# A hybrid decoder step on one core: token tiles normed in pairs, half of w_out split ahead into DRAM, output tiles beside attention's end

## The chip, the core and the metric

The kernel runs on one core of one Trainium2 chip. The metric is the device time of one execution in microseconds (us); lower is better. The engines are TensorE (PE, matmuls and transposes), VectorE (DVE), ScalarE (ACT), GpSimd (POOL) and SyncE (SP, which here only issues DMA transfers). Each engine works through its own instructions in order and waits on semaphores for the others.

## What is computed

One step of a decoder layer for a new sequence of 1024 tokens (d_model 1024) and for 8 sample tokens with a past of 2048, all in float32. In short:

```python
h = rms_norm(x, norm_g)
b_gate, c_gate, conv_in, z_conv, q, kv, gate_logits, z_attn = split(h @ w_in)
q = rope(rms_norm(q, q_gain)) / 8            # 8 heads of 64
k = rope(rms_norm(kv[..., 0, :, :], k_gain)) # 3 branches, 2 kv heads
o = g0 * attn(q, compress_blocks(kv_cmp)) + g1 * attn(q, top 16 blocks of kv_slc) \
    + g2 * attn(q, last 512 of kv_win)
y = x + concat(b_gate * short_conv(c_gate * conv_in) * silu(z_conv), o * silu(z_attn)) @ w_out
```

For the samples the compressed and selected branches read a paged cache through `page_table`. The key and value rows of the new tokens, the window state and the conv state are outputs too.

## The kernel before

**Matmuls.** A float32 operand is split into a high and a low part of type fp32r (`copy` on ACT makes the high part, `sub`, L78, on DVE or POOL the low part), and a product is three matmuls: high by high, high by low, low by high. `tok_mm` (L201) makes a tile of 128 tokens by 256 columns with 8 × 3 matmuls (L208 to L210), `chan_mm` (L216) a block of 128 channels by 384 tokens (L223 to L225). There are nine token tiles; the ninth holds the 8 samples.

**First stage.** `phase0` (L530) makes, in this order: the normed and transposed input `hH`, `hL` (`x_load`, `x_norm`, `turn_x`), the key and value rows of the compressed branch (weights `c0`), of the selected branch (`c1`), the compressed blocks of the new sequence (L599, from `XH`, `XL`), the rows of the window branch (`c2`), and the queries in two halves of 256 columns (`which`). `norm_rope` (L253) norms a tile's heads and turns them: squares on ACT (one instruction per head with accumulation for keys, one for a query tile, then a DVE reduction L259), the root in `rsqrt` (L189: one ACT and four small DVE steps, L194 to L197), and the products on DVE (L267, L270, L273, L275). `twice` (L277) doubles the keys into `kd`, and transposes put them into `K` (`k_finish`, L483) or, for the compressed branch, into `XH`, `XL` (`cmp_transposes`, L403). `posted` runs such work a set number of tiles later. Weights of the next pass are loaded on SP (`wraw`, L169) and split (`wh` on ACT, `wl` on POOL) while a pass runs. `x_load` has three buffers, so SP waits until a tile has been normed and transposed before it can load the fourth.

**Order of work.** `merge` (L30) interleaves two generators by the costs that they yield: `phase0` with weight 150 and `z_part`, blocks of the gate channels (`chan_stream`, L315), with weight `ZW` = 43. After that `first` (attention, then the output tiles) is merged with `second` (the other channel blocks and the convolution, `prefetch`, the sample's compressed cache, the sample's attention). A scheduler of the framework then places the instructions on the engines, which can move them past one another where data allows.

**Attention** (`attn_stream`, L754) has 32 units: 8 query tiles, 2 kv heads, 2 pairs of query heads. A unit makes scores on PE (L796), a masked softmax on DVE and ACT (L784, L786), scales the probabilities by a statistic and the gate on POOL (`scale`, L841 and L845), transposes them (L870), splits them into `ph`, `pl`, and multiplies by the values (L880). `finish` adds the result into `mixA`. The last units have the longest rows.

**Output.** `prefetch` (L1340) loads the eight pieces of the first half of `w_out` (`w_piece`, L1326, tile `wor`) and the compression weights `cwr`, and splits them on ACT and DVE, beside attention's last units. `out_stream` (L1360) makes 16 output tiles of 128 tokens by 512 columns, 24 matmuls each (L1405 to L1407), once attention is over; `cmp_stream` (L972) then gathers the sample's cache (L981, 16 indirect gathers of 1 MB through POOL's queue, two buffers), regroups it (`reg`), transposes (L999) and compresses it (L1023).

Of the kernel before, what the change touches and what calls it, by code (L numbers as in the profile page):

```python
# [1 line left out]

# [58 lines left out]
def hymba_step_kernel(ctx, tc, io):  # L61
    nc = tc.nc
    WARM = 24
# [55 lines left out]
    mixA = mixp.tile([128, 4, NTOK], F32, name="mixA")  # L119
    mCf = mixC.rearrange("p a c -> p (a c)")  # L120
# [3 lines left out]
    kv1p = left.enter_context(pool("kv1"))  # L124
    K, V = {}, {}

    K[1] = kv1p.tile([128, 2, 32 + SEQ], F32R, name="k1")
    kpc = K[1][:, :, 0:32]
    KOFF = {1: 32, 2: 0}
    V[1] = kv1p.tile([128, 8, 2, 128], F32R, name="v1")  # L130
# [16 lines left out]
    warm = ps.tile([128, 512], F32, name="cc", tag="cc", bufs=2)  # L147
    for _ in range(WARM):
        PE.matmul(warm[:, :256], vpc[:, 0], vpc.rearrange("p g c -> p (g c)"), start=True, stop=True)

    banks = {"mm": [(ps, "mm", 3)], "tp": [(ps, "tp", 3)], "cc": [(ps, "cc", 2)]}
# [9 lines left out]
    def w_loader(wp, n, kp, raw_bufs, hk, hl_bufs, lo_eng=POOL):  # L161


        def load(col, width):
            hs, ls, raws = [], [], []

            def fetch(i, home=wp):
                r = home.tile([128, kp, n], F32, name="wraw", bufs=raw_bufs)
                SP.dma_start(r[:, :, :width], w_in[:, i * kp:(i + 1) * kp, col:col + width])  # L169
                raws.append(r)  # L170

            def split(i, eh=ACT, el=lo_eng):
                for j in range(0, kp, hk):
# [4 lines left out]
                    sub(el, l[:, :, :width], r, f(h[:, :, :width]))  # L178
# [22 lines left out]
    def tok_mm(t, w, n):  # L201

        o = bank("mm")
# [47 lines left out]
    E2 = [(DVE, DVE), (DVE, DVE), (DVE, DVE), (DVE, DVE)]  # L251

    def norm_rope(wk, src, n, t, nh, ct, sn, ea=DVE, eb=DVE):  # L253
        w = nh * 64
        sq = wk.tile([128, 256], F32, name="sq")
        ss = wk.tile([128, 8], F32, name="ss", bufs=4)
        if nh == 4:
            ACT.activation(sq[:n, :w], src, AF.Square, scale=0.125)
            DVE.tensor_reduce(ss[:n, :nh], sq[:n, :w].rearrange("p (h d) -> p h d", h=nh), axis=AX, op=OP.add)  # L259
        else:  # L260
            for h in range(nh):
                c = slice(h * 64, h * 64 + 64)
                ACT.activation(sq[:n, c], src[:, c], AF.Square, scale=0.125, accum_out=ss[:n, h:h + 1])
        r = rsqrt(wk, ss[:n, :nh], n, nh)
        qn = wk.tile([128, 4, 64], F32, name="qn")
        q = qn[:n, :nh]
        DVE.tensor_tensor(q, src.rearrange("p (h d) -> p h d", h=nh), r[:, :, None].to_broadcast([n, nh, 64]), OP.mult)  # L267
        a = wk.tile([128, 4, 64], F32, name="ra")
        b = wk.tile([128, 4, 64], F32, name="rb")
        ea.tensor_tensor(a[:n, :nh], q, ct[:n, t][:, None, :].to_broadcast([n, nh, 64]), OP.mult)  # L270
        for i in range(2):
            o, s = slice(32 * i, 32 * i + 32), slice(32 - 32 * i, 64 - 32 * i)
            eb.tensor_tensor(b[:n, :nh, o], q[:, :, s],  # L273
                               sn[:n, t, o][:, None, :].to_broadcast([n, nh, 32]), OP.mult)
        DVE.tensor_tensor(src.rearrange("p (h d) -> p h d", h=nh), a[:n, :nh], b[:n, :nh], OP.add)  # L275

    def twice(wk, rows, n):  # L277

        kd = wk.tile([128, n, 2, 64], F32, name=f"kd{n}", tag="cwr" if n == 4 else "kd2", bufs=CWR if n == 4 else 3)
        v = rows[:, :n * 64].rearrange("p (a d) -> p a d", a=n)  # L280
        copy(DVE, kd, v[:, :, None, :].to_broadcast([128, n, 2, 64]))
        return kd

    def kv_rows(wk, o, t, br, ct, sn):

        if t < 8:
            n, src = 128, o
# [5 lines left out]
        if br == 2:  # L293
            copy(ACT, gates[:n, t, :], src[:n, 256:280])
# [1230 lines left out]
```

## Time and profile before

| | us |
|---|---|
| Median of 3 runs | 936.41 (935.55 to 942.97) |
| The profiled execution | 939.33 |
| Span of its profile, first to last instruction | 937.6 |
| Mean granted clock of TensorE in it | 0.976 of full speed |

Shares of busy time, stretches, waits and chains below are of the profiled execution, on the scale of its span, from 0 to 937.6 us. A busy PE is not PE at its peak, since matmuls overlap and their ends are modelled. In this execution the first key tile begins some 10 us in, the queries are made from about 170 to 236 us, attention runs to about 674 us, and the sample's stages with the output tiles follow.

### The profile page before, as it was taken

Reading aid. Unit: us, or ns where it says so; the run is one execution under the profiler, and the core shown is the slowest. Engines: PE = TensorE matmul, PEld = TensorE weight load, DVE = VectorE, ACT = ScalarE, POOL = GpSimd, SP = SyncE. Lnnn points to the kernel's source line nnn. Section 1 sums busy time; section 2 is a strip of 40 time slices with the busy share of each in tenths; the row PEclk is TensorE's granted clock in tenths of the full one; section 3 lists DMA queues with packets and bytes.
Section 4 is the critical chain, followed back from the end, with each engine's and each line's share of the span. In section 5 each row is a group of like instructions: output and inputs, shape, how many; then the busy total and the mean of one; then the engine's idle time right before and its main releaser. Section 6 shows DMA issues by size and latency. Waiting matters only on the chain.

```text
span 937.6 us, 16976 instructions
## 1 busy us (share of the span) xinstructions
PE 873.8 (93%) x5789; PEld 783.2 (84%) x5789; DVE 619.4 (66%) x1714; ACT 556.0 (59%) x1495; POOL 404.3 (43%) x550
## 2 busy tenths in 40 slices
PE   7988999999899999999989999999679999798998
PEld 6888999999689889898979899998568888576765
DVE  5896734788655555856775686577745555877883
ACT  5764543733665655656556666576757666675761
POOL 4132340311454444444434444343455543477761
PEclk8999989999999999999999999999989999899999
DMA  7513331211011000000000100001495661857631
GB/s 246 154 57 95 95 114 35 80 57 31 6 30 34 24 23 24 23 24 23 13 12 23 24 23 1 23 2 44 127 302 182 214 214 47 314 179 226 214 102 47
DMA packets 57955, 82.24 MB, mean 88 GB/s; under 512 B 14470, under 2 KB 43086, under 8 KB 55692
## 3 DMA queue, kind: packets, MB, share of 16 engines
q1 hardware_dynamic: 50956, 47.60, 16.9%
q0 software_dynamic: 6912, 33.56, 10.6%
q8 instruction: 46, 0.75, 0.3%
q14 instruction: 41, 0.34, 0.1%
HBM read 74.24 MB, written 11.10 MB: 91 GB/s over the span
## 4 chain that ended last, share of the span: by engine, by line
PE 49%; ACT 7%; DVE 7%; POOL 3%; issue 3%; DMA 1%; ACTq 0%; DVEq 0%; POOLq 0%
PE o L880 7%; PE pt L870 5%; PE s L796 5%; PE mm L225 5%; PE mm L224 5%; PE mm L223 5%; POOL P L845 2%; ACT P L786 2%; PE mm L1407 1%; PE pt L999 1%; PE mm L1405 1%; PE mm L1406 1%; PE mm L1023 1%; ACT ph L75 1%; PE o L1278 1%
## 5 line engine op out<-in xcount | busy, mean ns | idle before, releaser
L223 PE MATMUL mm<-hH,wh 128*128 128x384 f32 (+1 forms) x480 | 157.9, 329 | 0.0
L225 PE MATMUL mm<-hH,wl 128*128 128x384 f32 (+1 forms) x480 | 155.7, 324 | 0.0
L224 PE MATMUL mm<-hL,wh 128*128 128x384 f32 (+1 forms) x480 | 155.1, 323 | 0.0
L786 ACT ACTIVATE P<-P,stat 128x640 f32<-128x640 f32 (+7 forms) x192 | 112.9, 590 | 37.4 <-DVE stat L784 36.8
L79 POOL TENSOR_TENSOR wl<-wraw,wh 128x256 fp32r<-128x256 f32 (+1 forms) x120 | 87.7, 749 | 106.2 <-ACT wh L75 96.8
L79 DVE TENSOR_TENSOR pl<-pt,ph 128x512 fp32r<-128x512 f32 (+1 forms) x164 | 102.4, 636 | 45.3 <-ACT ph L75 43.9
L75 ACT ACTIVATE ph<-pt 128x512 fp32r<-128x512 f32 (+1 forms) x164 | 88.3, 549 | 66.1 <-PE pt L870 65.5
L845 POOL TENSOR_SCALAR P<-P,stat,gates 128x640 f32<-128x640 f32 (+7 forms) x128 | 101.1, 800 | 55.8 <-DVE stat L836 52.7
L870 PE MATMUL pt<-ident,P 128*128 128x128 f32 x592 | 95.5, 278 | 6.4 <-POOL P L845 3.5
L796 PE MATMUL s<-k,q 128*128 128x320 f32 (+8 forms) x416 | 95.8, 334 | 3.7 <-DVE q L79 1.5
L208 PE MATMUL mm<-wh,hH 128*128 128x256 f32 (+1 forms) x320 | 93.5, 292 | 0.4 <-ACT hH L75 0.4
L209 PE MATMUL mm<-wl,hH 128*128 128x256 f32 (+1 forms) x320 | 93.2, 292 | 0.2
L210 PE MATMUL mm<-wh,hL 128*128 128x256 f32 (+1 forms) x320 | 93.0, 291 | 0.0
L223 PEld LDWEIGHTS mm<-hH,wh 128*128 128x128 f32 x480 | 91.9, 191 | 0.8 <-DVE mixC L693 0.6
L224 PEld LDWEIGHTS mm<-hL,wh 128*128 128x128 f32 x480 | 91.9, 191 | 0.1
L225 PEld LDWEIGHTS mm<-hH,wl 128*128 128x128 f32 x480 | 91.9, 192 | 0.1
L784 DVE CUSTOM_DVE_ANT_0 P<-s,mask 128x32 f32<-128x32 f32 (+8 forms) x160 | 70.9, 473 | 27.0 <-PE s L796 22.4
L870 PEld LDWEIGHTS pt<-ident,P 128*128 128x128 f32 x592 | 70.0, 140 | 19.9 <-POOL P L845 10.1
L880 PE MATMUL o<-ph,v 128*128 128x256 f32 x264 | 74.5, 301 | 3.6 <-ACT ph L75 3.0
L880 PE MATMUL o<-pl,v 128*128 128x256 f32 x264 | 73.3, 300 | 3.3 <-DVE pl L79 3.2
L796 PEld LDWEIGHTS s<-k,q 128*128 128x128 f32 x416 | 66.8, 190 | 8.1 <-DVE q L79 1.7
L841 POOL TENSOR_SCALAR P<-P,stat,gates 128x32 f32<-128x32 f32 x64 | 22.9, 370 | 94.4 <-DVE stat L836 76.4
(342 smaller groups left out, 2182.9 us busy)
## 6 DMA issues: line engine op xcount, KB each, us to landing
wraw<-in_w_in_dram SPq DMA_DIRECT2D x56, 256.0 KB
xt<-in_x_prompt_dram SPq DMA_DIRECT2D x8, 512.0 KB
wor<-in_w_out_dram SPq DMA_DIRECT2D x16, 256.0 KB
xr<-in_x_prompt_dram SPq DMA_DIRECT2D x16, 256.0 KB
out_y_prompt_dram<-xr SPq DMA_DIRECT2D x16, 256.0 KB
sd<-in_state_win_kv_dram SPq DMA_DIRECT2D x8, 512.0 KB
out_s_win_dram<-in_state_win_kv_dram SPq DMA_DIRECT2D x8, 511.0 KB
cwr<-in_cmp_w_dram SPq DMA_DIRECT2D x32, 64.0 KB
```

Source lines behind the costliest of these rows:

```text
L75: return ACT.activation(out, in_, AF.Copy)
L79: return eng.tensor_tensor(out, a, b, OP.subtract)
L208: PE.matmul(o[:, :n], hH[t // 3][:, k, s], wh, start=k == 0, stop=False)
L209: PE.matmul(o[:, :n], hH[t // 3][:, k, s], wl, start=False, stop=False)
L223: PE.matmul(o[:, :n], wh, hH[c][:, k], start=k == 0, stop=False)
L224: PE.matmul(o[:, :n], wh, hL[c][:, k], start=False, stop=False)
L225: PE.matmul(o[:, :n], wl, hH[c][:, k], start=False, stop=k == 7)
L786: return lambda: ACT.activation(P, P, AF.Exp, bias=stt[:, 0, c:c + 1], scale=-1.0, accum_out=stt[:, 1, c:c + 1])
L796: PE.matmul(s[:, a:b], q[:, i], k, start=first, stop=not first)
L845: POOL.tensor_scalar(P[:, i, :n], P[:, i, :n], stt[:, 2, c + i:c + i + 1], gates[:, qi, gt:gt + 1], op0=OP.mult, op1=OP.mult)
L870: PE.transpose(p[:, y * 256 + i * 128:y * 256 + i * 128 + 128], src[:, i], ident)
L880: PE.matmul(o[0][:, :256], v, X[:, y * 256:y * 256 + 256], start=br == 1 and x == 0 and y == 0 and X is h[0], stop=last and y + 1 == len(p ...
```

## The change

**Pairs.** Two token tiles of a pass now share one PSUM bank (256 columns each). They are copied out together and normed together: `norm_rope` squares both in one ACT instruction, reduces on DVE, runs `rsqrt` once and makes products over twice the elements. `kd`, the values and the key transposes go by pairs, the transposes three tiles later instead of two. For the compressed branch the tokens are rearranged by four DMAs per pair (`token_pairs`), and one group of four transposes serves two tiles.

**Input.** Four x tiles are loaded into `mixA`, the others into buffers of their own, so that no load waits for a buffer. The squares are taken ahead (`x_stat`), tiles are normed three ahead, and `norm_g` is spread over the partitions by two matmuls instead of a 512 KB load. The low halves of some weights go alternately to POOL and DVE. `ENDS` (14000) is the cost yielded at the end of each pass, where the merge then places channel blocks; `ZW` is 42, `ZG` 3, the warm-up matmuls 8 instead of 24. By the order of the instructions PE runs 16 channel blocks ahead of attention's first transposes, 13 before.

**w_out.** During the queries the eight pieces of its first half are loaded, split and written to DRAM (`wo_d`). `prefetch` reads them back by eight DMAs on POOL's queue, fetches the compression weights on SP, and issues the first two gathers. `early_out` makes the output tiles of tokens 0 to 255, first half, in buffers that held queries; `first` waits for it before it closes attention's pools.

```diff
-    WARM = 24
+    WARM = 8
...
+    def norm_rope(src, n, t, ct, sn):
+        m, nh = src.shape[1:3]
...
+        ACT.activation(sq, src, AF.Square, scale=0.125)
+        DVE.tensor_reduce(ss, sq.rearrange("p i h d -> p (i h) d"), axis=AX, op=OP.add)
+        r = rsqrt(wk, ss, n, m * nh).rearrange("p (i h) -> p i h", i=m)
+        q = room("qn")
+        DVE.tensor_tensor(q, src, r[:, :, :, None].to_broadcast([n, m, nh, 64]), OP.mult)
+        DVE.tensor_tensor(src, q, ct[:n, t:t + m][:, :, None, :].to_broadcast([n, m, nh, 64]), OP.mult)
...
-    LAG, DEPTH, HK, HB, XB, ZW, CWR = 1, 2, 2, 4, 3, 43.0, 1
+    LAG, DEPTH, HK, HB, ZW = 1, 2, 2, 4, 42
...
-    ZG = 5
+    ZG = 3
...
+    def token_pairs(rows, t):
+        pr = prs[t // 2 % 2]
+        for i in range(2):
+            for r in range(2):
+                SP.dma_start(pr[i * 64:i * 64 + 64, :, r], rows[r::2, i * 256:i * 256 + 256].rearrange("p (a d) -> p a d", a=4))
+        return pr
...
+    def kv_tile_mm(t, w, n, br):
...
+            pair.append(tok_mm(t, w, n) if t % 2 == 0 else tok_mm(t, w, n, pair[0][:, 256:512]))
+            if t % 2:
+                o = pair[0]
+                pair[:] = [kv_room(br)]
+                copy(ACT, pair[0][1], o.rearrange("p (i j c) -> p i j c", i=2, j=2))
...
+            posts.append((lambda t=t: k_finish(br, t, kd), 3))
...
+        def w_split(k, l):
+            h = wk.tile([128, 512], F32R, name="kd2", bufs=2)
+            copy(ACT, h, f(l))
+            sub(DVE, l, f(l), f(h))
+            SP.dma_start(wo_d[k][:, 0], f(h))
+            SP.dma_start(wo_d[k][:, 1], f(l))
...
     def prefetch():
...
         for k in range(8):
+            w = wop.tile([128, 2, 512], F32R, name=f"wo{k}")
+            POOL.dma_start(w, wo_d[k])
+            wo[0, k] = w[:, 0], w[:, 1]
+            if k % 2 == 0:
+                if late:
+                    late(cw2)
+                late = cw_fetch(rawp, k // 2)
+            yield PREF
+        for i in range(2):
+            gather(i)
+            yield PREF
...
+    def early_out():
+        for t, homes in enumerate((("20", "00", "01", "10", "11"), ("11", "21", "00", "01", "10"))):
+            homes = [f"q{i}" for i in homes]
+            yield from out_tile(0, t, lambda name, dt: qkv.tile([128, 512], dt, name=homes.pop(0)))
...
     def first():
         yield from attn_stream()
+        while "early" not in done:
+            yield None
...
         yield from prefetch()
-        done["weights"] = True
+        yield from early_out()
+        done["early"] = True
```

How the order changes, at three places. The first is DVE in the query passes; before, a query tile (`q_...`) of 128 tokens:

```order
L259 TENSOR_REDUCE ss<-sq 128x4
L194 RECIPROCAL rs<-rs 128x4
L195 SCALAR_TENSOR_TENSOR rs<-ss,rs 128x4
L196 SCALAR_TENSOR_TENSOR rs<-rs 128x4
L197 SCALAR_TENSOR_TENSOR rs<-rs 128x4
L267 TENSOR_TENSOR qn<-q_1845,rs 128x256
L270 TENSOR_TENSOR ra<-qn,mixC 128x256
L273 TENSOR_TENSOR rb<-qn,mixC 128x4x32 x2
L275 TENSOR_TENSOR q_1845<-ra,rb 128x256
```

After, the same place, a pair of tiles, and behind it one low half of w_out (the tile `kd`, line 80):

```order
L263 TENSOR_REDUCE ss<-rb 128x8
L194 RECIPROCAL rs<-rs 128x8
L195 SCALAR_TENSOR_TENSOR rs<-ss,rs 128x8
L196 SCALAR_TENSOR_TENSOR rs<-rs 128x8
L197 SCALAR_TENSOR_TENSOR rs<-rs 128x8
L266 TENSOR_TENSOR qn<-q_1577,rs 128x512
L267 TENSOR_TENSOR q_1577<-qn,mixC 128x512
L271 TENSOR_TENSOR rb<-qn,mixC 128x8x32 x2
L273 TENSOR_TENSOR q_1577<-q_1577,rb 128x512
```

One run of steps over 512 columns now stands where two runs over 256 stood.

The second is POOL where attention ends (`P` is a unit's probabilities, scaled at L841 and L845; `ml` the low half of an output tile's input; `raw` a gather). Before, from the scalings of the last two units on:

```order
L845 TENSOR_SCALAR P_8550<-P_8550,stat,gates 128x640 x2
L845 TENSOR_SCALAR P_8749<-P_8749,stat,gates 128x1024 x2
L895 TENSOR_TENSOR mixA<-ot,mixA 128x128
L841 TENSOR_SCALAR P_3452<-P_3452,stat,gates 128x32 x2
L845 TENSOR_SCALAR P_8750<-P_8750,stat,gates 128x640 x2
L1363 MEMSET mS 128x320
L79 TENSOR_TENSOR ml<-mixC,mh 128x512
L895 TENSOR_TENSOR mixA<-ot,mixA 128x128
L79 TENSOR_TENSOR ml<-mixA,mh 128x512
L981 DMA raw<-in_cache_cmp_kv_dram,idx_c 128x2048 x2
L79 TENSOR_TENSOR ml<-mixC,mh 128x512
L79 TENSOR_TENSOR ml<-mixA,mh 128x512
```

After, from the longest scaling of the last unit but one to that of the last (the scalings are L970 and L974 there, `wo` the pieces of w_out read from `wo_d`, the gather L1107):

```order
L1474 DMA wo_8294<-wo_d_79 128x1024
L1474 DMA wo_8320<-wo_d_80 128x1024
L1024 TENSOR_TENSOR mixA<-ot,mixA 128x128
L1474 DMA wo_8322<-wo_d_81 128x1024
L1474 DMA wo_8331<-wo_d_82 128x1024
L970 TENSOR_SCALAR P_2980<-P_2980,stat,gates 128x32 x2
L974 TENSOR_SCALAR P_8069<-P_8069,stat,gates 128x640 x2
L1474 DMA wo_8342<-wo_d_83 128x1024
L1474 DMA wo_8351<-wo_d_84 128x1024
L1474 DMA wo_8366<-wo_d_85 128x1024
L1474 DMA wo_8400<-wo_d_86 128x1024
L974 TENSOR_SCALAR P_8268<-P_8268,stat,gates 128x1024 x2
```

The next instruction is the first gather (L1107 `raw`). Eight loads and the two gathers have moved in between the scalings; before, POOL issued no transfer until attention was over.

The third is PE at the same place. Before, the last products with the values (`o`, L880) and the first output matmuls (`mm`) behind them:

```order
L880 MATMUL o<-ph,v_1839 128x256
L880 MATMUL o<-pl,v_1839 128x256
L880 MATMUL o<-ph,v_1839 128x256
L880 MATMUL o<-pl,v_1839 128x256
L1405 MATMUL mm<-woh_8888,mh 128x512
L1406 MATMUL mm<-wol_8889,mh 128x512
L1407 MATMUL mm<-woh_8888,ml 128x512
L1405 MATMUL mm<-woh_8924,mh 128x512
```

After (values L1009, transposes of probabilities L999, output matmuls L1506 to L1508):

```order
L1508 MATMUL mm<-wo_8366,q_8449 128x512
L1009 MATMUL o<-pl,v_996 128x256
L1009 MATMUL o<-ph,v_996 128x256
L1009 MATMUL o<-pl,v_996 128x256
L999 MATMUL pt<-ident,P_8269 128x128 x4
L1009 MATMUL o<-ph,vpc 128x256
L1506 MATMUL mm<-wo_8400,q_8448 128x512
L1507 MATMUL mm<-wo_8400,q_8448 128x512
L1009 MATMUL o<-pl,vpc 128x256
L1009 MATMUL o<-ph,v_1573 128x256
L1009 MATMUL o<-pl,v_1573 128x256
L999 MATMUL pt<-ident,P_8269 128x128 x4
```

The first output tile's matmuls now stand between the last unit's transposes and products, and the second tile follows directly.

## Rows read from the trace of the kernel before

**Rows 1.** The page's first part: busy time, share of the span, instructions of each engine.

```profile
PE 873.8 (93%) x5789; PEld 783.2 (84%) x5789; DVE 619.4 (66%) x1714; ACT 556.0 (59%) x1495; POOL 404.3 (43%) x550
```

**Rows 2.** Stretches of the first 262 us: width, then busy time (instructions) by engine, clock, DMA.

```profile
0.00:20.00 20.00, 13.22 (x66) 11.16 (x66) 10.27 (x19) 11.24 (x29) 10.08 (x16) 0.89 0.67 226
20.00:40.00 20.00, 17.88 (x118) 17.68 (x119) 16.98 (x53) 13.49 (x39) 4.26 (x6) 0.85 0.64 189
40.00:64.00 24.00, 22.54 (x178) 21.32 (x176) 21.57 (x74) 15.04 (x49) 2.79 (x2) 1.00 0.24 79
64.00:82.00 18.00, 14.96 (x111) 14.39 (x111) 10.29 (x32) 10.50 (x39) 8.28 (x12) 0.91 0.22 58
110.00:138.00 28.00, 25.32 (x175) 24.68 (x174) 12.63 (x46) 13.64 (x53) 13.00 (x17) 0.82 0.41 120
170.00:236.00 66.00, 64.91 (x516) 64.55 (x516) 53.76 (x188) 30.95 (x89) 14.05 (x21) 1.00 0.19 54
236.00:262.00 26.00, 21.20 (x120) 17.18 (x119) 16.14 (x77) 17.93 (x62) 12.59 (x28) 0.93 0.08 21
```

**Rows 3.** What PE waited for in 0 to 236 us: total, times, longest (us).

```profile
PE tp L392 <- DVE xt L384: 5.5, 4, 1.9
PE tp L489 <- DVE kd L76: 3.7, 2, 2.0
PE tp L408 <- DVE kd L76: 3.0, 2, 1.9
```

**Rows 4.** Stretches at attention's end, columns as in the second group.

```profile
640.00:658.00 18.00, 17.59 (x130) 15.79 (x128) 15.11 (x37) 13.06 (x29) 5.28 (x7) 1.00 0.25 75
658.00:676.00 18.00, 11.50 (x76) 8.92 (x74) 14.98 (x33) 14.54 (x34) 7.37 (x9) 1.00 0.31 89
676.00:693.00 17.00, 15.12 (x68) 11.85 (x66) 6.29 (x8) 7.62 (x15) 12.23 (x13) 0.90 0.94 299
```

**Rows 5.** What PE waited for in 640 to 700 us, columns as above.

```profile
PE mm L1023 <- ACT xh L75: 3.0, 1, 3.0
PE o L880 <- DVE pl L79: 2.4, 4, 0.8
```

**Rows 6.** The chain that ended last, 640 to 700 us: start, duration, what.

```profile
687.32 7.20 DMA wor<-in_w_out_dram
```

**Rows 7.** DVE's groups by shape, 0 to 236 us: count | busy us, mean ns | idle before.

```profile
L267 DVE TENSOR_TENSOR qn<-rows,rs 128x128 f32<-128x128 f32 x24 | 9.2, 382 | 0.6
L267 DVE TENSOR_TENSOR qn<-q,rs 128x256 f32<-128x256 f32 x15 | 6.9, 457 | 0.4
L79 DVE TENSOR_TENSOR hL<-tp,hH 128x512 fp32r<-128x512 f32 x16 | 10.4, 686 | 2.9 <-ACT hH L75 2.8
L196 DVE SCALAR_TENSOR_TENSOR rs<-rs 128x2 f32<-128x2 f32 x24 | 6.5, 270 | 0.6
```

**Rows 8.** SP's queue, 0 to 21 us: start, duration, line, DMA.

```profile
9.80 8.64 SPq L373 DMA_DIRECT2D xt<-in_x_prompt_dram  x2
```

**Rows 9.** One of PE's groups by shape, 0 to 236 us.

```profile
L408 PE MATMUL tp<-ident,kd 128*128 128x128 f32 x32 | 5.0, 278 | 3.3 <-DVE kd L76 3.0
```

**Rows 10.** The tile wor of w_out: count, min/median/max ns, first to last start us.

```profile
L75 ACT ACTIVATE woh<-wor x16: 611/620/632, 656.9 to 815.8; 128x512 fp32r<-128x512 f32 x16
L79 DVE TENSOR_TENSOR wol<-wor,woh x16: 635/684/1356, 657.7 to 816.5; 128x512 fp32r<-128x512 f32 x16
```

**Rows 11.** The gathers, L981: min/median/max ns on POOL, and issue to landing.

```profile
L981 POOL DMA_INDIRECT raw<-in_cache_cmp_kv_dram,idx_c x16: 941/985/1260, 678.8 to 768.0; - x16
DMA to landing us min/median/max: 5.9/5.9/6.0
```

**Rows 12.** POOL's instructions, 636 to 680 us: start, duration, line, operation [idle before].

```profile
644.23 2.38 POOL L845 TENSOR_SCALAR P<-P,stat,gates 128x1024 f32<-128x1024 f32 x2 [6.68 <-DVE stat L836]
653.05 1.74 POOL L845 TENSOR_SCALAR P<-P,stat,gates 128x640 f32<-128x640 f32 x2
659.92 2.39 POOL L845 TENSOR_SCALAR P<-P,stat,gates 128x1024 f32<-128x1024 f32 x2 [5.13 <-DVE stat L836]
```

More of the change, by code (lines that the diff above doesn't have):

```diff
@@ L119, in hymba_step_kernel @@
     mixA = mixp.tile([128, 4, NTOK], F32, name="mixA")
+    dram = ctx.enter_context(pool("split", space=bass.MemoryType.DRAM))
+    wo_d = [dram.tile([128, 2, 512], F32, name=f"wo_d{k}") for k in range(8)]
     mCf = mixC.rearrange("p a c -> p (a c)")
@@ L380, in x_norm @@
         xt = xts.pop(t)[:n]
[L381 to L384 removed]
+        r = roots.pop(t)
+        for c in (slice(0, 512), slice(512, D)) if t == 0 else (slice(0, D),):
+            DVE.scalar_tensor_tensor(xt[:, c], xt[:, c], r, gps[:n, c], op0=OP.mult, op1=OP.mult)
         def turn_x():
@@ L528, in hymba_step_kernel @@
+    qp = []
+    qkv = None
     xcp2 = ExitStack()
+    rooms = prs = None
     def phase0():
+        nonlocal rooms, prs, qkv
+        ACT.dma_start(g1, io["norm_g"])
         x_load(0)
-        SP.dma_start(gbc, bcast_rows(io["norm_g"], D))
         SP.dma_start(idt, io["c_ident"])
+        for h in range(2):
+            PE.matmul(gps[:, h * 512:h * 512 + 512], one, g1[:, h * 512:h * 512 + 512], start=True, stop=True)
         c0 = wl0(COL_KV, 256)
         c0[1](0)
+        x_load(1)
         c0[1](1)
-        x_load(1)
@@ new lines, in phase0 @@
+            if t == 5:
+                tab1 = rope_tables(io["k_gain"][0, 1], 1, 1.0)
+                small_loads()
+            if t == 1:
+                for i in range(2):
+                    c1[1](i)
+                for i in range(2, 4):
+                    c1[1](i, xsp)
+            if t in (2, 3, 4, 5):
+                c1[2](t - 2, ACT, POOL)
+            if t == 7:
+                small_things()
+                cw_split = cw_fetch(wk, 0)
+            yield 3900 if t < 8 else ENDS
@@ L970, in cmp_rooms, with gather @@
         return cwp
+    raws = {}
+    def gather(n):
+        T, qd = divmod(n, 4)
+        r = rawp.tile([128, 2048], F32, name="raw", bufs=2)
+        POOL.indirect_dma_start(out=r, out_offset=None, in_=cache_cmp,
+                                in_offset=bass.IndirectOffsetOnAxis(ap=idx_c[:, T, qd:qd + 1], axis=0))
+        raws[n] = r
     def cmp_stream():
@@ L1005, in transposes @@
             return xh, xl
-        for n in range(2):
-            gather(n)
-        yield 12000
         regroup(0)
@@ new lines, in prefetch, with out_tile @@
+        for i in range(2):
+            gather(i)
+            yield PREF
+        late(cw2)
+        yield 0
+    begun = set()
+    def out_tile(n, t, room, made=None):
+        begun.add((n, t))
+        cols, s = slice(n * 512, (n + 1) * 512), slice(t * 128, t * 128 + 128)
+        xr = room("xr", F32)
+        SP.dma_start(xr, x_prompt[s, cols])
+        m = []
+        for src in (mixC, mixA):
+            mh, ml = (room(x, F32R).rearrange("p (k c) -> p k c", k=4) for x in ("mh", "ml"))
+            copy(ACT, mh, src[:, :, s])
+            sub(POOL, ml, src[:, :, s], f(mh))
+            m.append((mh, ml))
+        yield 0
+        o = bank("mm")
+        for k in range(8):
+            wh, wl = wo[n, k]
+            mh, ml = (x[:, k % 4] for x in m[k // 4])
+            PE.matmul(o, mh, wh, start=k == 0, stop=False)
+            PE.matmul(o, mh, wl, start=False, stop=False)
+            PE.matmul(o, ml, wh, start=False, stop=k == 7)
+            if k == 3:
+                yield 2600
+        DVE.tensor_tensor(xr, o, xr, OP.add)
+        SP.dma_start(y_prompt[s, cols], xr)
+        if made:
+            made()
+        yield 2600
```

565 lines of the change are left out of this document (288 added, 277 removed).

## The prediction

> **What bounds the kernel now.** I read the page's shares first, then tables of stretches, then what TensorE (PE) waited for, and last the chain of work where attention ends. The shares [rows 1] say that PE is busy 873.8 of 937.6 us and every other engine at most 66%. So PE's work is the floor, and only what PE loses can be won: time in which it stands idle, and time in which the granted clock is at the lower of its two levels (1.2 instead of 2.4 GHz).
>
> The stretches [rows 2] say where. For each I take width minus PE's busy time as idle, and (1 − clock) × width as what the clock took. 0–20 us: 6.8 + 2.2. 20–40: 2.1 + 3.0. 40–64: 1.5 + 0. 64–82: 3.0 + 1.6. 110–138: 2.7 + 5.0. 170–236, where the queries are made: 1.1. 236–262, where attention starts: 4.8 + 1.8. Together 35.6 us in 262, and the clock drops only in stretches that also have holes. The reader should see that VectorE (DVE) is the neighbour at its limit: 17.0 of 20, 21.6 of 24 and 53.8 of 66 us. PE's waits agree [rows 3]: 5.5 us for `xt` and 3.7 and 3.0 us for `kd`, all DVE's products.
>
> The second place is attention's end [rows 4]: 6.5 us idle in 658–676, 1.9 + 1.7 (clock) in 676–693, 0.4 before; a wait of 3.0 for `xh` follows at 696 [rows 5]. About 13.5 us. The chain there [rows 6] runs through 7.20 us of the w_out load `wor` and on to `woh`, `wol`, `xr`: the pieces of w_out come after attention, through ACT and DVE, which the last units of attention need too (2.4 us of PE's waits are for `pl` [rows 5]).
>
> **The change part by part.**
>
> *Pairs in the first stage.* DVE's time is mostly fixed per instruction: a product over 128x128 takes 382 ns, over 128x256 457, a subtraction over 128x512 686 [rows 7]. Two key tiles cost 2 × 382 per product, a pair 457. Three full products per tile for 24 tiles: 27.5 us before, 12 × 3 × 457 = 16.5 after. The four small steps of the root go from 24 × 4 to 12 × 4; at 270 ns at most that saves 13.0, and 12 reductions are added, no longer than such a product (5.5), since the accumulating squares go. For the queries 16 × 3 × 457 = 21.9 becomes 8 × 3 × 686 = 16.5, and 32 small steps go (8.6). Sum: 33 saved. Added are eight subtractions for w_out at 686 ns (5.5) and about 12 low halves of weights taken over from GpSimd (POOL) at 457 (5.5). Net about 22 us of DVE before attention, and the queries stay near 50 of 66 us with the w_out work in them.
>
> What PE gets of that is estimated by stretch. 0–20: the first tile still has to be loaded, squared and normed; the 512 KB broadcast of norm_g is gone and weights no longer stand behind a held x load (SP stood 8.64 us there [rows 8]); 3 of 9.0. 20–40: the tiles are loaded early and normed three ahead; 3.5 of 5.1. 40–64: 0.5 of 1.5. 64–82: the `kd` copies of the first branch go to DMAs; 3 of 4.7. 110–138: the key transposes are asked for three tiles later, channel matmuls are kept for the pass's end, and the clock should stay up with the hole filled; 5.5 of 7.7. Nothing elsewhere. Sum 15.5; from below 0 (the holes move), from above 25 (all but the first load and norm). I take the middle because a pair's chain is longer than a tile's, and each pass still ends with a chain that no tile of its own covers.
>
> *Fewer transposes.* 16 of 32 go; 32 are busy 5.0 us [rows 9], so at most 2.5; I take 2. The 24 − 8 warm-up matmuls stand ahead of the first data and are worth nothing; the two matmuls that spread norm_g cost nothing there, but if x came first they would cost under 1 us.
>
> *Attention's start.* Three channel blocks go ahead of attention (its tables and masks move too): 2 of 6.6 us, from 0 to 4. The blocks are missing as filler later, where two output tiles come in.
>
> *w_out ahead.* The eight splits (620 ns ACT, 684 DVE each [rows 10]) leave 640–700 for the query stage: 5.0 us of ACT and 5.5 of DVE in a place where PE waits for these engines. The 16 writes and 8 loads to and from DRAM issue on queues, behind no matmul.
>
> *Attention's end.* The POOL order shows what is new: eight loads of 512 KB and two gathers between the last scalings of probabilities. The trace has no such load; the nearest row is the gather of 1 MB: POOL is held 941 to 1260 ns, median 985, and it lands 5.9 us later [rows 11]. Eight issues are about 8 us of POOL, which is busy 5.3 and 7.4 of 18 us there [rows 4]. Two loads follow the scaling that starts at 644, four stand between the one at 653.1 and the one at 659.9 [rows 12]: 653.1 + 1.7 + 4 × 0.985 = 658.7, so the second is not delayed, with 1.2 us to spare (0.1 at 1260 ns). At the gather's pace 4 MB need 23.6 us: begun at about 646.6, they have landed at 670. The output matmuls stand between the last matmuls of attention (PE's order), so they fill the 6.5 us and put the clock right; the gathers are issued 11 to 16 us earlier than at 678.8 [rows 11]. If all is hidden, 12 of 13.5 us come back; if the loads are late, PE's order makes attention wait: down to −10. I take 9, less 1 for POOL: 8.
>
> One rule speaks against this. In the rows POOL's issue takes 985 ns beside a busy DVE. The Trainium skill (SBUF — State Buffer, Reading the diagram and the part on bandwidth pools) says that a DMA issued from GpSimd has its descriptors written by its cores, which a DVE operation on the shared port locks out; about 620 ns alone become 3100. By that, four issues would end at 667 instead of 658.7, and the gain at the end would be about nothing: 917 in place of 909. The longest of 16 issues in this trace is 1260 ns, so the rows do not bear it out for gathers; no run here shows it for plain loads.
>
> **Sum.** Against the profiled execution of 939.33 us: 15.5 + 2 + 2 + 8 = 27.5, so 911.8. That execution is 2.9 above the median 936.41, so the forecast is 909.
>
> **Rivals.**
> (a) All the holes close: 25 + 2 + 4 + 12 = 43, so 893. For it: DVE's relief is larger than the holes it makes. Against: DVE stays near 50 of 66 us, and pairs are late by one tile.
> (b) Only one of the two places gains. Most likely it is the first stage alone: the issues on POOL take longer than 1.26 us each and hold the scalings of attention's last unit and the matmuls behind them, 8 lost, 15.5 + 2 + 2 kept: 917, chance 0.13. For it: the margin is 1.2 us over four issues. Against: the longest of 16 gathers was held 1260 ns. (The rule of the port, above, is this case.) The end alone, 8 + 2 + 2 less 1 for longer chains: 925, chance 0.07.
> (c) The change does not reach what PE waits for: in 20–64 the loads rather than DVE set the pace, DVE's saving falls where it was idle, and the output tiles only move from after attention into it. Transposes and start remain, 4: 932. Against: the waits name DVE.
> (d) Slower: SP's queue. SP issues in order, and the copies of token pairs (four per pair) and the stores wait for a pair's whole chain on DVE; weights and rope tables are queued behind them. The one hold of this kind now is 8.64 us [rows 8]. Weights of the next pass are asked for about three tiles ahead; the 18 query tiles fill 66 us, so three are 11 us, and from a hold of 11 us on PE starves. With a loss of 8.64 beyond it at four places (two key passes, two query halves): 35 lost, none of the 15.5 gained: 939.3 − 12 + 35 = 962, less 2.9: 959.
>
> **How the numbers follow.** Forecast 0.50, (a) 0.15, (b) 0.20, (c) 0.08, (d) 0.07. A measurement of this kernel can tell about 1% from no change, which is below 927 or above 946. Faster takes the forecast, (a) and nine tenths of (b): 0.83. Same: the rest of (b) and (c): 0.10. Slower: 0.07. The range reaches from (a) to just past the upper end of (b): 892 to 930.
>
> **What would show it.** PE idle plus clock loss before 236 us should fall from 29 to about 14 in the stretches counted, with DVE well under 21.6 us in the stretch that was 40–64 and no wait of PE on `kd` over 1 us. Stage by stage, the end of the queries should come 17 to 18 us earlier, attention itself should take as long as before, and the first gather should be issued ahead of attention's last matmul. POOL's `wo` issues at about 1 us each and no wait of PE for `wo` show the end right; issues of 3 us, or a scaling of probabilities queued behind them, show the rule of the port right. Wrong would be: weights that PE waits for after 64 us (d), holes as large with DVE idle (c), or a gain that is all on one side of 262 us (b).

## The result and the profile after

The changed kernel takes 944.35 us (median, 940.99 to 948.74, 20 runs); the kernel before, on the same chips, 939.17 (934.28 to 943.48, 20 runs). The ratio is 1.0065 with a 95% interval of 1.0050 to 1.0081: it is slower by 0.65%, where 909 us was forecast. (By the prediction's own bounds, 927 to 946 us, it counts as the same.) The profiled execution after has a span of 945.0 us and a mean clock of 0.966, against 937.6 and 0.976.

The busy shares of the page, which answer to [rows 1], say nothing of the cause: DVE has 27 us less to do, PE is busy 8.5 us longer. The mean clocks account for about that much: 3.4% of 945.0 is 32.1 us, against 2.4% of 937.6, 22.5.

```profile
PE 882.3 (93%) x5761; PEld 790.0 (84%) x5761; DVE 592.0 (63%) x1513; ACT 528.9 (56%) x1329; POOL 397.2 (42%) x538
```

To find the place, I follow one event through the traces: the doubling of a unit's queries, two transposes per unit, whose row gives the start of the first and of the last of 64. First the kernel before, then after (count, min/median/max ns, first to last start).

```profile
L768 PE MATMUL pt<-ident,qd x64: 270/272/328, 235.8 to 647.1; 128*128 128x128 f32 x64
```

```profile
L897 PE MATMUL pt<-ident,qd x64: 270/272/421, 258.5 to 663.8; 128*128 128x128 f32 x64
```

Attention starts at 258.5 us instead of 235.8 and its last unit at 663.8 instead of 647.1. From there to the end it is 290.5 us before (937.6 − 647.1) and 281.2 after (945.0 − 663.8). So the end of the kernel gained 9.3 us and everything ahead of attention's last unit lost 16.7; the start of attention alone comes 22.7 us later. The stretches of [rows 2] after the change:

```profile
0.00:20.00 20.00, 15.46 (x68) 11.89 (x69) 9.75 (x23) 11.47 (x25) 9.33 (x16) 1.00 0.78 271
20.00:40.00 20.00, 13.88 (x90) 13.41 (x89) 14.05 (x31) 9.72 (x21) 5.20 (x6) 0.83 0.54 164
40.00:64.00 24.00, 23.54 (x180) 22.20 (x180) 13.06 (x42) 8.53 (x20) 1.42 (x1) 1.00 0.30 73
64.00:82.00 18.00, 17.18 (x134) 16.49 (x133) 9.61 (x33) 8.58 (x24) 11.70 (x14) 1.00 0.36 93
110.00:138.00 28.00, 23.11 (x146) 22.62 (x146) 13.69 (x38) 6.27 (x24) 7.64 (x9) 0.76 0.34 107
170.00:236.00 66.00, 62.79 (x478) 61.96 (x477) 45.04 (x106) 24.84 (x58) 9.01 (x11) 0.95 0.27 86
236.00:262.00 26.00, 20.13 (x110) 18.43 (x109) 10.74 (x29) 9.17 (x22) 5.39 (x11) 0.93 0.51 157
```

DVE did get its relief: 13.1 us in 40–64 where it had 21.6. PE's loss, idle plus clock as in the prediction, is 4.5, 9.5, 0.5, 0.8, 11.6, 6.5 and 7.7 us in these seven stretches, 41.1 together; it was 35.6. Up to 236 us, where the prediction wanted about 14 in place of 29, it is 33.4. PE's waits name the holes (0 to 300 us; what was waited for, then total us, times, longest):

```profile
PE tp L409 <- DVE xt L401: 6.1, 1, 6.1
PE mm L223 <- DVE mixC L806: 5.9, 4, 2.1
PE gps L702 <- DVE kc L707: 4.9, 1, 4.9
PE mm L208 <- ACT wh L76: 2.2, 1, 2.2
```

The second, four waits for `mixC`, is the place where attention should start. Of ACT's instructions there, the copies of the pieces (`kd`) and the readouts of channel blocks (`mixC`; start, duration, operation, idle before):

```profile
234.98 0.62 ACT L76 ACTIVATE kd<-kd 128x512 fp32r<-128x512 f32 x1
238.60 0.49 ACT L805 ACTIVATE mixC<-mm 128x384 f32<-128x384 f32 x1 [1.44 <-PE mm L225]
242.83 0.63 ACT L76 ACTIVATE kd<-kd 128x512 fp32r<-128x512 f32 x1 [3.74 <-DMA kd<-in_w_out_dram]
244.51 0.49 ACT L805 ACTIVATE mixC<-mm 128x384 f32<-128x384 f32 x1 [1.04 <-PE mm L225]
248.23 0.63 ACT L76 ACTIVATE kd<-kd 128x512 fp32r<-128x512 f32 x1 [3.23 <-DMA kd<-in_w_out_dram]
254.54 0.63 ACT L76 ACTIVATE kd<-kd 128x512 fp32r<-128x512 f32 x1 [4.18 <-DMA kd<-in_w_out_dram]
256.94 0.49 ACT L805 ACTIVATE mixC<-mm 128x384 f32<-128x384 f32 x1 [1.77 <-PE mm L225]
```

and of SP's queue, loads of the pieces of w_out (L748), their writes to DRAM (L755, L756) and the masks (L877):

```profile
238.13 0.34 SPq L756 DMA_DIRECT2D wo_d<-kd  x1
240.08 0.33 SPq L748 DMA_DIRECT2D kd<-in_w_out_dram  x1
243.49 0.32 SPq L755 DMA_DIRECT2D wo_d<-kd  x1
244.22 0.32 SPq L756 DMA_DIRECT2D wo_d<-kd  x1
245.59 0.33 SPq L748 DMA_DIRECT2D kd<-in_w_out_dram  x1
249.61 0.32 SPq L756 DMA_DIRECT2D wo_d<-kd  x1
251.36 0.46 SPq L748 DMA_DIRECT2D kd<-in_w_out_dram  x1
255.92 0.33 SPq L756 DMA_DIRECT2D wo_d<-kd  x1
256.35 1.84 SPq L877 DMA_DIRECT2D mask<-in_c_mask_dram  x4
```

Four of the eight pieces are split after the queries. Each needs both buffers of `kd2`, one for the raw piece, which becomes the low part, and one for the high part, so a load goes out only 1.4 to 2.0 us after the last write was issued, and ACT stands 3.2 to 4.2 us for it. The load of attention's masks (L877) comes right after the last write. PE meanwhile does channel blocks; a block needs a bank that ACT and DVE have read out. Its four waits:

```profile
240.03 0.44 PE L223 MATMUL mm<-hH,wh 128*128 128x384 f32 x1 [1.46 <-DVE mixC L806]
245.64 0.39 PE L223 MATMUL mm<-hH,wh 128*128 128x264 f32 x1 [1.17 <-DVE mixC L806]
250.88 0.44 PE L223 MATMUL mm<-hH,wh 128*128 128x384 f32 x1 [2.06 <-DVE mixC L806]
258.07 0.44 PE L223 MATMUL mm<-hH,wh 128*128 128x384 f32 x1 [1.17 <-DVE mixC L806]
```

Only the third stands behind the copy of a piece: its readout, at 249.99 us, follows the copy at 248.23 and four splits of weights. Before the second and the fourth, ACT itself had waited for PE (1.04 and 1.77 us in ACT's rows), so these are the bare way from PE over ACT and DVE back to PE; the first stands behind DVE's products for the last pair of queries. So ACT's waits for the loads are not themselves PE's holes; what moved is the place in PE's order where attention begins, behind more channel blocks. In 259–300 PE's clock is 0.79. The stretch of the last query tiles and that of attention's start, first after the change, then before (columns as in [rows 2]):

```profile
196.00:232.00 36.00, 32.79 (x240) 32.00 (x239) 22.97 (x57) 9.49 (x21) 0.73 (x1) 0.91 0.21 68
259.00:300.00 41.00, 37.84 (x193) 31.86 (x192) 23.22 (x114) 25.93 (x98) 20.31 (x45) 0.79 0.06 14
```

```profile
196.00:232.00 36.00, 36.00 (x294) 35.70 (x293) 30.83 (x101) 14.42 (x43) 9.12 (x14) 1.00 0.15 42
259.00:300.00 41.00, 39.83 (x263) 36.95 (x264) 22.22 (x93) 25.91 (x92) 21.74 (x45) 1.00 0.10 26
```

Before, the same 41 us at attention's start had clock 1.00, and the last query tiles lost nothing where they now lose 3.2 idle and 3.2 of clock.

### The profile page after: what moved, and what is told of

The parts are those of the page before. It is cut to its first block, busy times and chain, and to the rows that moved or that the text cites. A ratio compares the mean times of both kernels' runs of the same rounds, so it can differ in the third digit from the quotient of the medians.

```text
span 945.0 us, 16596 instructions
## 1 busy us (share of the span) xinstructions
PE 882.3 (93%) x5761; PEld 790.0 (84%) x5761; DVE 592.0 (63%) x1513; ACT 528.9 (56%) x1329; POOL 397.2 (42%) x538
## 4 chain that ended last, share of the span: by engine, by line
PE 61%; DVE 14%; ACT 9%; DMA 5%; issue 4%; POOL 4%; SPq 2%; ACTq 0%; DVEq 0%; POOLq 0%
PE o L1009 7%; PE mm L223 6%; PE mm L225 6%; PE pt L999 6%; PE mm L224 6%; PE s L925 5%; PE mm L210 3%; PE mm L209 3%; PE mm L208 3%; POOL P L974 2%; ACT P L915 1%; PE mm L1150 1%; PE pt L1129 1%; ACT ph L76 1%; PE mm L1506 1%
## 5 line engine op out<-in xcount | busy, mean ns | idle before, releaser
L80 POOL TENSOR_TENSOR wl<-wraw,wh 128x256 fp32r<-128x256 f32 (+1 forms) x105 | 77.8, 760 | 167.6 <-ACT wh L76 150.0
L974 POOL TENSOR_SCALAR P<-P,stat,gates 128x640 f32<-128x640 f32 (+7 forms) x128 | 100.3, 794 | 54.6 <-DVE stat L965 52.8
L999 PE MATMUL pt<-ident,P 128*128 128x128 f32 x592 | 97.6, 282 | 6.9 <-POOL P L974 3.4
L925 PE MATMUL s<-k,q 128*128 128x320 f32 (+8 forms) x416 | 97.9, 337 | 0.7 <-DVE stat L964 0.4
L999 PEld LDWEIGHTS pt<-ident,P 128*128 128x128 f32 x592 | 71.5, 142 | 21.0 <-POOL P L974 10.0
L1009 PE MATMUL o<-ph,v 128*128 128x256 f32 x264 | 75.5, 304 | 1.6 <-ACT ph L76 1.2
L1009 PE MATMUL o<-pl,v 128*128 128x256 f32 x264 | 74.5, 304 | 1.6 <-DVE pl L80 1.5
L208 PEld LDWEIGHTS mm<-wh,hH 128*128 128x128 f32 x320 | 62.8, 196 | 4.8 <-ACT wh L76 2.4
```

Source lines behind the costliest of these rows:

```text
L80: return eng.tensor_tensor(out, a, b, OP.subtract)
L208: PE.matmul(o[:, :n], hH[t // 3][:, k, s], wh, start=k == 0, stop=False)
L925: PE.matmul(s[:, a:b], q[:, i], k, start=first, stop=not first)
L974: POOL.tensor_scalar(P[:, i, :n], P[:, i, :n], stt[:, 2, c + i:c + i + 1], gates[:, qi, gt:gt + 1], op0=OP.mult, op1=OP.mult)
L999: PE.transpose(p[:, y * 256 + i * 128:y * 256 + i * 128 + 128], src[:, i], ident)
L1009: PE.matmul(o[0][:, :256], v, X[:, y * 256:y * 256 + 256], start=br == 1 and x == 0 and y == 0 and X is h[0], stop=last and y + 1 == len(p ...
```

## The experiments

Theory S is that the split pieces, through their two buffers, hold attention. Two theories stood against it: C, that the channel blocks kept for the end of a pass hold attention (the diff puts them there by ENDS), and P, that the chain of a pair does. G is a theory on the hole at 119 us, the wait for `kc`. On the chips of the experiments the kernel before took 937.4 to 939.7 us (medians), so the difference of two medians from different chips is uncertain by 1 to 2 us.

**e1: four rooms.** The pieces take turns in memory of `mixC` that no longer holds tables.

```diff
+        def spare(i):
+            a = (0, 512, 1152, 1664)[i]
+            return mCf[:, a:a + 512].bitcast(F32R)
...
-            l = wk.tile([128, 512], F32R, name="kd2", bufs=2)
+            l = spare(2 * (k % 2))
...
-            h = wk.tile([128, 512], F32R, name="kd2", bufs=2)
+            h = spare(2 * (k % 2) + 1)
```

> Edit: the w_out pieces split in the query passes take turns in four rooms of 512 columns in mixC that hold no table any more, instead of the two buffers of kd2. Theory S (each piece needs both buffers, so the next load waits until the last write to DRAM has landed, and the four pieces left after the queries hold attention's start): the eight pieces are split before 232 us, attention's first doubling of queries (L897) stands near 238 us instead of 258.5, the granted clock of the 40 us behind it is above 0.9 instead of 0.79, and the time falls by 10 to 17 us, to 927 to 934. Rival C (the channel blocks that ENDS keeps for the end of a pass hold attention): within 3 us of 944. Rival P (the chain of a pair of queries is what attention waits for): within 3 us of 944.

Measured: 927.58 us (924.41 to 931.68), ratio to before 0.9886 (0.9847 to 0.9925). Attention starts at 232.9 us and the stretch behind it runs at clock 1.00. The doubling's row, and the two stretches as above, both of e1:

```profile
L901 PE MATMUL pt<-ident,qd x64: 270/272/328, 232.9 to 644.9; 128*128 128x128 f32 x64
```

```profile
196.00:232.00 36.00, 35.28 (x275) 34.77 (x274) 28.26 (x69) 14.05 (x32) 4.99 (x7) 1.00 0.24 74
259.00:300.00 41.00, 40.04 (x268) 37.75 (x267) 20.68 (x86) 24.44 (x85) 20.80 (x42) 1.00 0.11 27
```

16.8 us of the loss were these two buffers. By the stretches, 5.7 of it lie in the last query tiles (6.4 lost after the change, 0.7 here) and 10.8 at attention's start (11.8 and 1.0). S stands; C and P, which expected 944, fall. In the instruction order of this kernel the channel matmuls ahead of attention's first transposes go back from 129 to 101 per line (104 before): the extra blocks stood in attention's place only while the pieces were late.

**e2: no split in the queries.** The eight pieces are loaded and split in `prefetch`.

```diff
-                elif wsp:
-                    w_split(*wsp)
...
-            POOL.dma_start(w, wo_d[k])
+            x = r[:, k % 4 * 512:k % 4 * 512 + 512]
+            SP.dma_start(x, w_out[:, k, 0:512])
+            pieces.append((k, x))
+            if len(pieces) > 2:
+                w_half(*pieces.pop(0))
```

> Edit: no piece of w_out is split in the query passes; prefetch loads the eight pieces into the buffers of the first two gathers and splits them there on ACT and DVE; the gathers follow the splits, and the two output tiles stay beside attention's end. Theory S: attention starts near 238 us as in e1, so the first 300 us are as short as in e1 or up to 3 us shorter (5.0 us of ACT and 5.5 of DVE less in the queries); the end pays up to 6 us of it back, as the splits stand beside attention's last units again: 928 to 938 us. Rivals C and P: attention starts near 258 us, and the time is 944 or more.

Measured: 932.16 us (931.39 to 932.96). The queries end 3.1 us earlier than in e1 (last query product at 223.9 and 227.0 us, one execution each; e8 shows that this can scatter by as much), attention starts at 233.1, and the whole is 4.6 us longer than e1. So the splits cost more beside attention than in the queries, and the idea of moving them was right; the first gathers, which here follow the splits, may have a part in the 4.6 us.

**e3: no blocks kept for the last pass.**

```diff
-                yield ENDS if t == 7 else 1300
+                yield ENDS if t == 7 and which == 0 else 1300
```

> Edit: the cost yielded at the end of the last query pass is 1300 instead of ENDS (14000), so the merge keeps no channel blocks for that place. Rival C: the blocks ahead of attention go from 129 to about 104 matmuls per line, attention starts near 240 us, and the time falls by 10 us or more. Theory S: attention still waits for the last piece of w_out, starts at 255 us or later, and the time stays within 3 us of 944.

Measured: 944.87 us (940.16 to 948.42), attention's start at 259.4. Nothing changed: the channel matmuls ahead of attention stay at 129 per line, so the edit did not remove the blocks, and ENDS in the last pass is not what puts them there. With e1, where ENDS is as it was and the blocks are gone, C is out.

**e4: two banks for the compressed blocks.**

```diff
-            o = gps[:, j * 512:j * 512 + 512]
+            o = gps[:, 0:512] if j == 0 else bank("mm")
```

> Edit: the second half of the compressed blocks (L702) goes to a bank of its own instead of the second half of the tile gps, as it was before the change. Theory G (the two halves share one tile, so the second half's first matmul waits until DVE has read the first, which stands behind a pair's chain): the wait of 4.9 us at 119 us goes, the granted clock of 110 to 138 rises from 0.76 to above 0.9, and the queries end 6 to 10 us earlier; the whole time falls by 3 to 10 us, less if attention's start stays where the split pieces hold it. Rival: the wait only moves to the next reader of DVE's result, and less than 2 us is gained before 200 us.

Measured: 938.38 us (936.39 to 941.15), 6.0 below the changed kernel. The wait for `kc` is gone and PE is busy all through 110–138, where it was for 23.1 of 28 us; the clock comes only to 0.82, not above 0.9:

```profile
110.00:138.00 28.00, 28.00 (x182) 27.73 (x181) 14.66 (x39) 7.30 (x27) 8.19 (x9) 0.82 0.37 112
```

The queries end at 225.7 instead of 231.0, a little less than G expected. G stands: before, each half had a tile of its own (`bank("cc")`); the change put both halves into one tile, and the second half's matmuls waited for DVE's readout of the first, which stood behind the chains of a pair and of the sample.

**e5: e1 and e4 together.**

> Edit: e1 (four rooms for the w_out pieces) and e4 (a bank of its own for the second half of the compressed blocks) together. If the two losses are separate, the gains add: 944.4 - 16.8 - 6.0 = 921.6, so 919 to 924, with attention's start near 227 to 228 us. If the place of the compressed blocks was only ahead of a stretch in which PE would wait anyway, the time is that of e1, 927.6.

Measured: 921.92 us (921.18 to 925.07), ratio to before 0.9816 (0.9778 to 0.9854). The gains add. This version beats both kernels. It still has the hole at 28 us, PE's longest wait in the first 300 us:

```profile
PE tp L409 <- DVE xt L401: 6.1, 1, 6.1
```

**e6: single roots.** On e5:

```diff
-            if t in (0, 2):
-                x_stat(t + 4, t + 5)
-            elif t == 4:
-                x_stat(8)
+            if t < 5:
+                x_stat(t + 4)
```

> Edit: e5, and the squares and roots of the x tiles 4 to 7 one by one instead of by two. Theory X (the 6.1 us hole at 28 us is tile 4 waiting for tile 5's squares and the shared root): the hole shrinks by 1.5 to 4 us and the time falls by 1 to 4 us against e5. Rival (the hole is ACT and DVE being behind PE's own products, or the load): the hole stays within 1 us, the time within 1.5 us of e5.

Measured: 928.56 us (926.54 to 930.14), 6.6 longer than e5. The hole shrinks from 6.1 to 4.6 us, the least that X (the pair's roots make it) expected, but the order moved elsewhere: a wait of 2.7 us for POOL's `qn` appears at 70 us, where e5 has 0.8, and the queries end at 225.0 instead of 219.5. What the hole alone is worth stays open.

```profile
PE tp L409 <- DVE rs L194: 4.6, 1, 4.6
PE tp L484 <- POOL qn L476: 2.7, 1, 2.7
```

**e7: no early output tiles.** On e1; it computes the two tiles with the others, after attention.

```diff
-    EARLY, PREF = 2, 400
+    EARLY, PREF = 0, 400
...
-        yield from early_out()
```

> Edit: e1 without the two output tiles beside attention's end; they come with the other output tiles after it, as before the change; the pieces of w_out still come from DRAM and the first two gathers still go ahead. Theory E (the tiles fill PE where attention's last units leave it idle): the stretch of 28 us ahead of attention's last product loses its 11 us of output matmuls and shortens by only 2 to 5 us, and the time rises by 4 to 9 us over e1, to 932 to 937. Rival (the pieces ready early and the early gathers make the gain, the tiles would be filler later anyway): within 3 us of e1.

Measured: 934.32 us (931.51 to 942.73, 10 runs), 6.7 above e1. PE at attention's end, the stretch 658 to 676, in e1 and then in e7:

```profile
658.00:676.00 18.00, 17.39 (x104) 14.19 (x103) 10.24 (x25) 10.20 (x25) 10.19 (x11) 1.00 0.70 217
```

```profile
658.00:676.00 18.00, 13.49 (x67) 10.80 (x68) 9.19 (x21) 10.99 (x26) 11.27 (x14) 0.81 0.67 196
```

Without the tiles PE is idle 4.5 of 18 us, and the clock falls to 0.81. Theory E, that the early tiles fill attention's end, stands.

**e8: late gathers.** On e1, the first two gathers are issued by `cmp_stream` again.

> Edit: e1 with the first two gathers issued by the compressed stage itself, after attention, as before the change. Theory E: the first product of the compressed cache comes 5 to 10 us later, but the output tiles fill PE meanwhile, and the time rises by 0 to 4 us. Rival (the gathers are what starts the stage): it rises by 6 us or more, which is most of the end's gain.

Measured: 934.05 us (928.69 to 937.67). By the median that is the rival's 6 us. The trace tells otherwise: attention starts at 238.4 against e1's 232.9, though both kernels have the same instruction order up to there. PE falls behind e1's execution in four places: 1.4 us by 35 us, 0.4 near 110, 1.5 between 162 and 172 and 2.3 between 193 and 210. In 170–180 and in 205–215 e8's clock is 0.83, e1's 1.00. So 5.5 us at attention's start can come from one execution to the next. From the last unit's start (651.5) to the end (935.9) it is 284.4 us, against 281.6 in e1. The same sum gives 285.2 for e7, and 280.5 to 283.1 in the eight kernels whose end is that of the change (the change itself, e1, e3 to e6, e9, e10). So the gathers are worth some 1 to 4 us and the early tiles 2 to 5, one execution each; that is inside what E expected of the gathers, and the spread of the start hides it in the median.

**e9: two rooms.** e1 with two of the four rooms: the chain is serial again, but no longer lies in the pool `w0`.

```diff
-            l = spare(2 * (k % 2))
+            l = spare(2)
...
-            h = spare(2 * (k % 2) + 1)
+            h = spare(3)
```

> Edit: e1 with two rooms in mixC instead of four, so that a piece of w_out still needs both rooms and the next load waits for the last write to DRAM, but no transfer of a piece lies in the pool w0 any more, whose memory attention's tables and the convolution's buffers take over. It splits theory S in two. S1 (the chain through two buffers is late by itself): four pieces are still split after 230 us and the time is 938 to 944. S2 (attention waits for the memory of the pool, which the late pieces hold): attention starts near 233 us and the time is within 4 us of e1, 924 to 932, wherever the last pieces are split.

Measured: 938.18 us (936.27 to 940.32), between the two. Attention starts at 239.8, though pieces are split at 237, 246, 256 and 265 us (of ACT's copies):

```profile
188.68 0.63 ACT L76 ACTIVATE mixC<-mixC 128x512 fp32r<-128x512 f32 x1 [3.85 <-DMA mixC<-in_w_out_dram]
237.37 0.62 ACT L76 ACTIVATE mixC<-mixC 128x512 fp32r<-128x512 f32 x1
246.41 0.63 ACT L76 ACTIVATE mixC<-mixC 128x512 fp32r<-128x512 f32 x1 [1.22 <-DMA mixC<-in_w_out_dram]
255.76 0.62 ACT L76 ACTIVATE mixC<-mixC 128x512 fp32r<-128x512 f32 x1
```

So both halves of S have a part. S1's signs came, four pieces after 230 us and a time at the edge of its range; S2's time did not, but attention no longer waits for the last pieces. Where the pieces lie is worth 6.2 us of the 16.8 (944.4 − 938.2), and that there are two rooms instead of four the other 10.6 (938.2 − 927.6). How the late chain costs the 10.6 us is traced in part only. In 200–220 PE loses 4.0 us idle and 3.4 of clock here, in e1 0.5 and none; its one wait over 1 us there is for weights of the last query pass:

```profile
PE mm L208 <- ACT wh L76: 2.7, 1, 2.7
```

ACT splits these weights at 202.3 us, behind a pair's squares at 200.4 that had waited 3.4 us for DVE. In e1 it splits them at 198.5, ahead of those squares, and PE waits 0.2 us.

**e10: more work for DVE.** On e5, two more products per `norm_rope` into a scratch that nobody reads.

```diff
         DVE.tensor_tensor(src, src, b, OP.add)
+        for _ in range(2):
+            DVE.tensor_tensor(q, b, b, OP.mult)
```

> Edit: e5 with two more products of DVE per norm_rope, over the whole pair, into the scratch qn, which nobody reads: 12 pairs of 256 elements and 8 of 512 and the 5 sample tiles, 2 x 457 and 2 x 686 ns each, some 24 us of DVE before attention, as much as the pairs took from it. Theory D of the prediction (DVE's time sets the pace of the first stage): the queries end 10 us or more later and the time rises by 8 to 20 us, to 930 to 942. Theory L (once tiles go in pairs PE's losses before attention are single holes and the clock behind them, and DVE has room): less than 4 us, 918 to 926.

Measured: 933.35 us (931.15 to 934.70), 11.4 above e5. D has the time right, L the passes. Up to 220 us DVE is busy 153.8 us, as much as before the change (152.6) and 13.4 more than in e5, yet the last query product starts at 220.3 instead of 219.5: PE's products within the passes no longer follow DVE's time. The 11.4 us come after: the squares of the last pairs wait for the single scratch `rb`, and attention starts at 242.2 instead of 225.4. From 199.7 us on the squares of a pair follow those of the pair before by 6.8 us (199.7, 206.5, 213.3), always waiting for DVE, so the norms have fallen behind PE, and attention waits for them. The edit does two things: it adds work to DVE, and as its products read `rb` it holds that scratch longer. Which of them delays attention was not tried. The stretch up to 220 us in e10, then in e5, and ACT's last squares in e10 with the time that they waited for DVE:

```profile
0.00:220.00 220.00, 208.18 (x1510) 201.23 (x1511) 153.80 (x397) 93.58 (x234) 51.86 (x67) 0.96 0.42 131
```

```profile
0.00:220.00 220.00, 206.63 (x1517) 199.12 (x1518) 140.44 (x373) 96.15 (x239) 53.45 (x67) 0.97 0.42 131
```

```profile
224.71 0.63 ACT L262 ACTIVATE rb<-q 128x512 f32<-128x512 f32 x1 [3.38 <-DVE qn L275]
233.66 0.63 ACT L262 ACTIVATE rb<-q 128x512 f32<-128x512 f32 x1 [5.28 <-DVE qn L275]
```

## Why the prediction was wrong

**The step that failed** is the one on w_out: "The 16 writes and 8 loads to and from DRAM issue on queues, behind no matmul", priced at nothing. Its ACT and DVE time was counted (10.5 us, and most of it was hidden: e2 gains only 3.1 us up to the queries' end by leaving it out). Not counted was the wait inside: load, copy, subtraction, write, next load, all through two buffers, with ACT waiting in order for each load. It cost 16.8 us (e1), 6.2 of them by where the buffers lie (e9). The diff shows `bufs=2` in both lines, and SP's rows show each load behind the writes of the piece before; I named SP's queue as rival (d), but for weights, and did not follow the chain of the pieces. By which waits the rest of the 16.8 us reaches PE stays open in part.

**110–138 us, 5.5 expected, nothing had.** The loss there was 7.7 and became 11.6. The bank that the change took away was in the diff too (`bank("cc")` became half of `gps`), and the prediction does not mention it: 6.0 us (e4).

**0–40 us, 6.5 expected.** Loss 14.1 before, 14.0 after. The tiles are loaded early, but their squares stand in ACT's order behind the first tiles' work (those of tiles 4 and 5 at 23.1 and 24.6 us, their common root at 26.1), and the wait for tile 4 is one hole of 6.1 us instead of four smaller ones. **40–82, 3.5 expected:** 6.1 became 1.3, better than forecast; here the waits for `kd` did go.

**Why the 15.5 us were too many.** I took the waits for DVE's products as DVE being at its limit and credited its relief to PE. The relief was sized right: up to 220 us DVE is busy 22.8 us less (152.6 to 129.8), against a net of 22. PE did not get it. e10 shows that in these kernels PE's products in the passes do not follow DVE's total, though the norms of the last queries, which attention waits for, came later with more of it. That the waits were chains in order, made longer by pairs, fits the hole at 28 us (e6); for the others it is argued, not shown. In e5, with both mistakes undone, the queries end 11.9 us earlier than before (231.4 to 219.5), where the prediction had 17 to 18; after the change alone it was 0.4 (231.0). At the last unit's start 9.4 us are left (647.1 to 637.7). That is the size of the first stage's whole gain, transposes and attention's start with it, where 19.5 was forecast.

**Attention's start, 2 expected.** The three channel blocks ahead of it, which I counted as a gain, were the sign of the loss. With the pieces in four rooms, or in two outside the pool, they are gone (101 and 102 matmuls per line).

**Attention's end, 8 expected, 9.3 had.** This term was right in mechanism, and in size as far as one execution of each kernel tells: e7 shows that the tiles fill PE and hold the clock (2 to 5 us by its trace, 6.7 by the medians), and by e8 the gathers add some 1 to 4 us. POOL's price was lower than I took, median 564 ns per load instead of 985:

```profile
L1474 POOL DMA_DIRECT2D wo<-wo_d x8: 537/564/763, 663.2 to 673.0; - x8
DMA to landing us min/median/max: 3.8/4.7/6.9
```

PE waited 0.4 us for a piece in all. The scaling of the last unit starts at 677.5 us, 13.7 after that unit's doubling, against 12.8 before. The loads did not hold it up, since POOL had stood idle for 3.9 us, waiting for DVE:

```profile
677.49 2.66 POOL L974 TENSOR_SCALAR P<-P,stat,gates 128x1024 f32<-128x1024 f32 x2 [3.89 <-DVE stat L965]
```

No load took over 763 ns beside a DVE busy 14.2 of 18 us (658–676), and no gather over 1049. The rule of the shared port in the Trainium skill (SBUF — State Buffer, Reading the diagram and A bandwidth-pool intuition that's wrong (but worth ruling out)), which I took to make an issue 3100 ns, gives that figure for an issue beside a copy on DVE. The trace does not test it: between the first and the last of these loads DVE's one copy took 0.16 us.

**The rivals.** The second form of (b), the end alone, names what came: the end gained 9.3 us. It had a chance of 0.07 and the time 925, because it put the loss of the first stage at 1 us and kept 2 us each for the transposes and for attention's start; 16.7 us were lost ahead of attention's last unit. I gave the other form, the first stage alone, nearly twice that. (c), that DVE's relief falls where PE does not wait for it, holds for 0–40 us, though not by its reason: the waits there still name DVE, not the loads. (d) had the right kind of mechanism, transfers in order behind others, at the wrong transfers. By the prediction's bounds the result counts as the same, for which 0.10 was too little with a serial chain that I had not followed to its end.

## What to carry to other kernels

When work is moved into a place with room, follow its whole chain through its buffers, transfers included: with two buffers per item, both needed at once, every item costs a full round trip, and an engine that works in order can carry that wait to whoever stands behind it. When a diff shares a tile that two users had to themselves, ask who reads the first half and when. An instruction order in which filler stands where the next stage should begin was here a sign that the stage waits; look for what it waits for before counting the filler as a gain.

## What was not expected

The clock can cost more than the waits that go with it. In 259–300 us no single wait of PE exceeds 1 us in the changed kernel and 3.2 us are idle in all, yet 8.6 us are lost to the clock (0.79 of 41), after the four holes of 1.2 to 2.1 us between 238 and 258 us. In e1, without those holes, the same stretch has 1.00; which of the holes count was not tried. With the same instruction order up to attention, e8's profiled execution ended its queries 5.5 us later than e1's (232.5 against 227.0); up to 220 us the two are idle alike (18.1 and 18.6 us), and the mean clock is 0.93 against 0.95. And DVE's total, which I took for the limit of the passes, is not the limit of PE's products in them: 13.4 us more of it moved the last query product by 0.8 us, and attention's start by 16.8 (e10).
